# First mixer of a two-layer trunk: one adaLN unit with each product unit, in place of three with two

## The chip, the core and the metric

The kernel runs on one core of one Trainium2 chip. The metric is the device time of one execution in microseconds (us). Three timed executions of the kernel before took 2756.81, 2764.85 and 2773.1 us; the median, 2764.85 us, is the time before. A further execution was recorded by the hardware profiler, and every duration below is from it.

## The reference

The reference is a two-layer decoder trunk on one sequence of 256 tokens with 2048 channels, all in 32-bit floats. Each layer has a token mixer and a SwiGLU block, and each of these four sub-layers is

`x <- LayerNorm(ALPHA * x + (1 + gate(c)) * f(x * (1 + scale(c)) + shift(c)))`

The shift, scale and gate come from a conditioning vector c ("adaLN"):

```
mod = jax.nn.silu(c) @ w + b
shift, scale, gate = jnp.split(mod, 3, axis=-1)
```

For each sub-layer w has 2048 rows and 6144 columns, 48 MB in all, and is read once. The first layer's mixer (the "first mixer" here) projects its input to the columns of two head groups, an mLSTM group (8 heads of 128) and an RWKV-7 group (16 heads of 64), runs both recurrences, and sends their concatenated output through one more projection. The second layer's mixer does the same with retention and gated DeltaNet.

## The kernel before

**Product units.** Every large projection is cut into products of 512 output columns, and a product into units. A unit is one 1 MB load of weights (128 partitions x 2048 floats, 8 KB in each partition) into a tile called raw. Both halves of the tile are then split into two parts of reduced precision: ScalarE writes the high part hi (line 713), VectorE subtracts it to get the low part lo (line 714). TensorE multiplies hi and lo with the activations, split likewise, in 24 matmuls of 512 columns per unit (lines 728 to 730, eight of each). A mixer product has four units. `raw_p` has three tiles and the hi and lo parts have three buffers each.

**adaLN units.** The 48 MB of each adaLN matrix is cut into 48 units of 1 MB, 192 for the four sub-layers, numbered 0 to 191. A unit is the weights of 128 output columns, transposed. Its computation is one VectorE instruction on the whole tile (line 649), which multiplies it with silu(c) and sums along each row. So an adaLN unit costs one load of 1 MB and one long VectorE instruction, and neither ScalarE nor TensorE. Where an adaLN unit's tile is taken from is set by `self.homes`. In the first mixer this is `("raw",)`: the adaLN units share the three raw tiles with the weights of the products. In the later stages they go to two tiles of their own, za and zt (FFN), or alternate between za and raw (second mixer).

**Where adaLN units are put.** After each product unit `product` calls `fill(rate)`:

```
self.ada_credit = getattr(self, "ada_credit", 0.0) + rate
while self.ada_credit >= 0.999 and self.ada_next < self.ada_limit:
    self.ada(1)
    self.ada_credit -= 1.0
```

So `rate` is the number of adaLN units per product unit, up to a limit on their number. Units 0 to 31 (shift and scale of the first sub-layer) are read in `first_products`, before the mixer. In `mixer_ab` the limit is 80: it reads units 32 to 47 (the first gate) and 48 to 79 (shift and scale of the second sub-layer). The gate is first needed by `gate_rows` in `mix_out`, the others by `norm` at its end; both call `ada` for whatever is still missing by then.

**The first mixer.** `mixer_ab` has twelve products of four units, 48 product units. Eight of them belong to `rwkv` and its callback `after`: four give the remaining columns of the RWKV heads, four give columns for the first four mLSTM heads, which are put by in DRAM ("by", line 1151) and fetched again (line 1158). Between them four batches of RWKV heads run, each with a chain of small VectorE steps (the inverse, lines 1012 to 1024) and small matmuls; the fourth goes side by side with the first mLSTM group. The last four products belong to the second mLSTM group, a generator that `mix_out` steps through before its own products with `o_ab`, whose rate is 0.

**Order.** The Python order of the calls is the program order. Within a pool, tiles are opened in the order of the program. At the end of `body` a planner (`Plan`) simulates the engines with estimated costs and writes one fixed order for each engine, the loads on SyncE's queue included: among the instructions that could start it takes the one with the smallest priority, which is its place in the program, less an advance of 2000 for a weight's load and split. All of this is done when the program is built.

Of the kernel before, what the change touches and what calls it, by code (L numbers as in the profile page):

```python
# [1895 lines left out]
def body(tc, ins, out):  # L1896
    with ExitStack() as stack:
        k = Trunk(tc, ins, out, stack)
        k.setup()
        k.ada_limit = 32  # L1900
        h, early = k.first_products()
        x = (ins["x"], None)
        k.ada_limit = 80
        side = k.mixer_ab(h, 48.0 / 32, early)
        x, h = k.mix_out(ins["o_ab"], x, 0, side)
        x, h = k.ffn(0, x, h)
        k.ada_limit = 176
        k.mixer_cd(h, 32.0 / 44)
        x, h = k.mix_out(ins["o_cd"], x, 2)
        k.ffn(1, x, h)  # L1910
        plan = Plan(tc, tc.nc, 250, k.after)
        plan.prepare(0)
        order, _ = plan.run([x.bass_priority for x in plan.ins])
        plan.impose(order)
# [18 lines left out]
```

## Time and profile before

| | before |
|---|---|
| timed runs, median (lowest to highest) | 2764.85 us (2756.81 to 2773.1) |
| the profiled execution's own time | 2755.91 us |
| span of its instructions | 2754.2 us |
| TensorE (PE) busy | 2627.3 us, 95% |
| VectorE (DVE) busy | 2005.0 us, 73% |
| ScalarE (ACT) busy | 1272.4 us, 46% |
| mean granted TensorE clock | 0.982 |

The profile is a page of one execution. It gives the busy time of each engine, that of 40 slices of the span, the chain of work that ended last, and groups of instructions: source line, engine, operation, output<-inputs by tile name, count, busy time, the mean duration in ns, and the idle time of the engine just before. The trace behind it answers questions on a stretch of time: the busy time of each engine (windows), who waited for whom (waits), and the instructions that touch a tile. PE is TensorE's matmuls, PEld its weight loads, SPq SyncE's queue of loads. Matmuls overlap, so a busy PE need not be a PE at its peak.

### The profile page before, as it was taken

The numbers are of one execution on the slowest core, as the hardware profiler recorded it, in microseconds if no ns is written. First come the engines' busy times: TensorE is split into PE (matmuls) and PEld (weight loads), VectorE is DVE, ScalarE is ACT, GpSimd is POOL, SyncE is SP. The second block draws the span as 40 slices with busy tenths as digits, with TensorE's granted clock in tenths as the row PEclk, the third lists the DMA queues.
The fourth block names the chain that finished last, engine by engine and source line by source line (L and its number), as shares of the span: only waits on it lengthen the run. The fifth ranks groups of instructions, "written<-read, shape, count | busy, mean of one in ns | idle before, by whom it ended". The sixth has DMA issues, their size and how long they took to land.

```text
span 2754.2 us, 33686 instructions
## 1 busy us (share of the span) xinstructions
PE 2627.3 (95%) x12906; PEld 2155.3 (78%) x12906; DVE 2005.0 (73%) x3153; ACT 1272.4 (46%) x1706; POOL 76.8 (3%) x88
## 2 busy tenths in 40 slices
PE   5598999999999999999999999999999999999997
PEld 3476777788788888888888888888778888888886
DVE  7899887658777777767767989875866664557457
ACT  2364545557644444434446654444354444443442
POOL 0000100110000000000000101000000000000000
PEclk9899999999999999999999999999999999999999
DMA  9988775226578888778856776665657675556554
GB/s 394 358 297 300 253 287 207 92 93 211 202 302 303 311 320 315 286 251 309 311 194 227 272 282 220 259 231 204 226 200 274 259 271 188 196 213 240 192 186 165
DMA packets 109819, 681.60 MB, mean 247 GB/s; under 512 B 12437, under 2 KB 15705, under 8 KB 31577
## 3 DMA queue, kind: packets, MB, share of 16 engines
q1 hardware_dynamic: 108506, 677.36, 67.0%
q8 instruction: 101, 1.65, 0.2%
q10 hardware_dynamic: 1152, 2.10, 0.2%
q14 instruction: 60, 0.49, 0.0%
HBM read 668.89 MB, written 10.52 MB: 247 GB/s over the span
## 4 chain that ended last, share of the span: by engine, by line
PE 75%; DVE 6%; issue 3%; DMA 3%; ACT 2%; POOL 0%; DVEq 0%; SPq 0%; ACTq 0%; POOLq 0%
PE g L730 23%; PE g L728 23%; PE g L729 23%; DVE lo L714 1%; PE m L974 1%; ACT hi L713 1%; DMA t<-x 1%; DMA t<-lnrow 1%; DMA za<-ada 1%; DVE raw L649 0%; PE m L1254 0%; PE m L909 0%; PE c L1432 0%; DVE t L870 0%; DMA raw<-w_ab 0%
## 5 line engine op out<-in xcount | busy, mean ns | idle before, releaser
L714 DVE TENSOR_TENSOR lo<-raw,hi 128x1024 fp32r<-128x1024 f32 (+2 forms) x802 | 972.4, 1215 | 594.1 <-ACT hi L713 589.6
L713 ACT ACTIVATE hi<-raw 128x1024 fp32r<-128x1024 f32 (+2 forms) x802 | 842.3, 1053 | 1117.1 <-PE g L730 1028.5
L728 PE MATMUL g<-hi,h 128*128 128x512 f32 (+2 forms) x2312 | 908.8, 394 | 53.7 <-ACT h L792 39.5
L729 PE MATMUL g<-lo,h 128*128 128x512 f32 (+2 forms) x2312 | 907.0, 392 | 4.6 <-DVE lo L714 4.6
L730 PE MATMUL g<-hi,h 128*128 128x512 f32 (+2 forms) x2312 | 905.7, 392 | 0.0
L728 PEld LDWEIGHTS g<-hi,h 128*128 128x128 f32 x2312 | 439.3, 190 | 148.4 <-ACT h L792 42.4
L729 PEld LDWEIGHTS g<-lo,h 128*128 128x128 f32 x2312 | 440.2, 190 | 97.1 <-DVE lo L714 8.8
L730 PEld LDWEIGHTS g<-hi,h 128*128 128x128 f32 x2312 | 439.6, 190 | 86.6 <-issue 2.0
L728 PE MATMUL g<-hi,a 128*128 128x512 f32 x920 | 361.0, 392 | 5.8 <-DVE t L870 5.8
L729 PE MATMUL g<-lo,a 128*128 128x512 f32 x920 | 359.9, 391 | 0.5 <-DVE lo L714 0.5
L730 PE MATMUL g<-hi,a 128*128 128x512 f32 x920 | 359.8, 391 | 0.0
L728 PEld LDWEIGHTS g<-hi,a 128*128 128x128 f32 x920 | 173.4, 189 | 42.1 <-DVE t L870 6.3
L729 PEld LDWEIGHTS g<-lo,a 128*128 128x128 f32 x920 | 173.5, 189 | 36.2 <-DVE lo L714 0.9
L730 PEld LDWEIGHTS g<-hi,a 128*128 128x128 f32 x920 | 173.4, 188 | 35.8
L649 DVE SCALAR_TENSOR_TENSOR raw<-raw,silu_c 128x2048 f32<-128x2048 f32 x82 | 187.4, 2286 | 16.5 <-DMA raw<-ada 8.7
L649 DVE SCALAR_TENSOR_TENSOR za<-za,silu_c 128x2048 f32<-128x2048 f32 x56 | 127.9, 2284 | 3.5 <-DMA za<-ada 3.5
L649 DVE SCALAR_TENSOR_TENSOR zt<-zt,silu_c 128x2048 f32<-128x2048 f32 x38 | 86.8, 2284 | 1.4 <-DMA zt<-ada 1.4
L1438 DVE SCALAR_TENSOR_TENSOR f<-c,cols_sb,f 128x253 f32<-128x253 f32 (+2 forms) x120 | 56.1, 475 | 3.0 <-ACT f L1435 2.4
L1639 POOL TENSOR_SCALAR s<-cons_sb,log_alpha 128x128 f32<-128x128 f32 x16 | 15.9, 1006 | 1008.6 <-DVE log_alpha L1583 867.6
L649 DVE SCALAR_TENSOR_TENSOR a<-a,silu_c 128x2048 f32<-128x2048 f32 x16 | 36.4, 2286 | 0.2
L912 ACT ACTIVATE t<-m,affine 128x128 f32<-128x128 f32 x96 | 34.9, 470 | 0.1
L1254 PE MATMUL m<-y 64*128 64x256 f32 x128 | 30.6, 413 | 3.6 <-DVE a L1257 3.4
(480 smaller groups left out, 2095.7 us busy)
## 6 DMA issues: line engine op xcount, KB each, us to landing
raw<-gu SPq DMA_DIRECT2D x176, 1024.0 KB, 4.7
raw<-dn SPq DMA_DIRECT2D x88, 1024.0 KB, 4.8
raw<-ada SPq DMA_DIRECT2D x82, 1024.0 KB, 5.4
raw<-w_cd SPq DMA_DIRECT2D x60, 1024.0 KB, 4.8
za<-ada SPq DMA_DIRECT2D x56, 1024.0 KB, 7.0
raw<-w_ab SPq DMA_DIRECT2D x48, 1024.0 KB, 5.0
zt<-ada SPq DMA_DIRECT2D x38, 1024.0 KB, 6.9
a<-ada SPq DMA_DIRECT2D x16, 1024.0 KB, 17.0
```

What stands on the lines that cost most here:

```text
L649: v.scalar_tensor_tensor(w[:], w[:], 1.0, self.sc[:], ALU.mult, ALU.mult, accum_out=m[:, i:i + 1])
L713: nc.scalar.activation(hi[:, :2 * n], ws, AF.Copy)
L714: nc.vector.tensor_tensor(lo[:, :2 * n], ws, hi[:, :2 * n], ALU.subtract)
L728: mm(o, ah, wh, start=start and k == 0, stop=False)
L729: mm(o, ah, wl, start=False, stop=False)
L730: mm(o, al, wh, start=False, stop=stop and k == 3)
L912: nc.scalar.activation(h32[:, j, :], b[:, P * j:P * j + P], AF.Identity, bias=self.ab[:, sub + 1, 16 + k:17 + k], scale=self.ab[:, sub + 1 ...
L974: nc.tensor.transpose(b[:, P * k:P * k + P], gs[:, t, P * k:P * k + P], self.ident)
L1254: mm(b[:, T * x:T * x + T], bk[r, c, x, t, :], ar[r, c, t].rearrange("p x s -> p (x s)"), start=True, stop=True)
L1438: v.scalar_tensor_tensor(o[:, d:T], b[:, T * j:T * j + T - d], self.col(wname, 4 * (tile0 + i + j) + 3 - d), o[:, d:T], ALU.mult, ALU.add)
L1639: nc.gpsimd.tensor_scalar(L[:], sl, self.gl[:, t, 4 * g + j:4 * g + j + 1], None, ALU.mult)
```

## The change

One number in `body`: the rate at which the first mixer takes adaLN units goes from 48/32 to 48/48. Before, 1.5 units stand behind each of the first 32 product units (the first eight products), and none behind the other 16. After, one unit stands behind each of the 48 product units. The limit of 80, the tiles, the loads and the computation are the same, and the rates of the later stages are not touched. The planner makes its order anew.

```diff
         k.ada_limit = 80
-        side = k.mixer_ab(h, 48.0 / 32, early)
+        side = k.mixer_ab(h, 48.0 / 48, early)
         x, h = k.mix_out(ins["o_ab"], x, 0, side)
```

## The prediction

> **What bounds the kernel now.** I read the page first, then, since the change touches one stage only, the stretches of that stage.
>
> ```profile
> PE 2627.3 (95%) x12906; PEld 2155.3 (78%) x12906; DVE 2005.0 (73%) x3153; ACT 1272.4 (46%) x1706; POOL 76.8 (3%) x88
> ...
> GB/s 394 358 297 300 253 287 207 92 93 211 202 302 303 311 320 315 286 251 309 311 194 227 272 282 220 259 231 204 226 200 274 259 271 188 196 213 240 192 186 165
> ```
>
> TensorE is busy for 95% of the span, so over the whole kernel only 5% (127 us) is idle. The traffic is uneven: the third to sixth of the 40 slices (138 to 413 us) move 253 to 300 GB/s, the eighth and ninth (482 to 620 us) 92 and 93. Which products lie where, and which adaLN units, is told by two rows of groups of lines, from 140.8 to 447.2 us and from 447.2 to 620 us, and by the loads of the two tensors:
>
> ```profile
> L730 PE MATMUL g<-hi,h 128*128 128x512 f32 x256 | 104.7, 409 | 0.0
> ...
> L649 DVE SCALAR_TENSOR_TENSOR raw<-raw,silu_c 128x2048 f32<-128x2048 f32 x46 | 105.0, 2283 | 6.1 <-DMA raw<-ada 5.9
> L649 DVE DVE_READ_ACCUMULATOR raw<-raw,silu_c 128x1 f32 x46 | 3.7, 81 | 0.0
> ...
> L730 PE MATMUL g<-hi,h 128*128 128x512 f32 x128 | 52.1, 407 | 0.0
> ```
> ```profile
> L690 SPq DMA_DIRECT2D raw<-ada x48: 327/328/360, 124.2 to 433.1; - x48
> L690 SPq DMA_DIRECT2D raw<-w_ab x48: 327/328/371, 120.7 to 588.9; - x48
> ```
>
> A product unit has eight matmuls of line 730, so the first stretch ("early") holds 32 product units, the first eight products, and the second ("late") the other 16. All 48 adaLN loads are issued by 433.1 us, 46 of them computed in the early stretch, none in the late. How the two stretches stand, cut finer, with a stretch of the FFN below for comparison:
>
> ```profile
> core 0: us, PE busy (x) PEld busy (x) DVE busy (x) ACT busy (x) POOL busy (x), PEclk, DMA share, GB/s
> 140.80:192.00 51.20, 49.18 (x232) 37.96 (x231) 46.37 (x87) 32.09 (x52) 0.00 (x0) 1.00 0.84 294
> 192.00:262.00 70.00, 59.47 (x251) 44.37 (x250) 64.66 (x129) 28.52 (x46) 5.85 (x5) 0.95 0.83 309
> 262.00:315.00 53.00, 52.07 (x405) 41.84 (x404) 44.16 (x94) 25.48 (x53) 6.32 (x5) 1.00 0.69 248
> 315.00:385.40 70.40, 64.94 (x393) 50.15 (x392) 65.92 (x140) 33.45 (x54) 0.79 (x2) 0.98 0.82 296
> 385.40:447.20 61.80, 59.34 (x309) 45.38 (x307) 43.24 (x113) 27.05 (x58) 4.38 (x5) 0.94 0.60 217
> 447.20:485.90 38.70, 37.70 (x307) 30.89 (x308) 28.35 (x85) 25.18 (x40) 0.00 (x0) 1.00 0.56 190
> 485.90:523.00 37.10, 32.68 (x171) 24.16 (x170) 22.85 (x93) 17.02 (x47) 7.33 (x11) 0.87 0.10 29
> 523.00:555.00 32.00, 32.00 (x171) 27.23 (x170) 25.65 (x67) 22.28 (x33) 0.00 (x0) 0.99 0.48 165
> 555.00:617.00 62.00, 60.92 (x452) 50.90 (x451) 37.12 (x109) 29.62 (x57) 7.57 (x12) 1.00 0.29 103
> ...
> 140.80:447.20 306.40, 285.01 (x1584) 219.71 (x1582) 264.34 (x559) 146.58 (x262) 17.34 (x16) 0.97 0.76 274
> 447.20:617.00 169.80, 163.29 (x1097) 133.18 (x1098) 113.97 (x353) 94.11 (x175) 14.89 (x23) 0.97 0.34 118
> ...
> 826.00:1500.00 674.00, 670.33 (x3051) 555.49 (x3050) 490.60 (x548) 302.25 (x343) 0.00 (x0) 1.00 0.76 281
> ```
>
> Early, PE idles 306.4 - 285.0 = 21.4 us and DVE is 86% busy (92 to 94% in the two stretches of 70 us); late, PE idles 6.5 us and DVE is 67% busy. What PE waits for early is in the waits:
>
> ```profile
> PE g L728 <- ACT hi L713: 10.3, 6, 3.0
> PE g L729 <- DVE lo L714: 3.0, 6, 0.5
> PE m L1254 <- DVE a L1257: 3.0, 4, 1.9
> PE c L1202 <- DVE za L1105: 1.4, 2, 1.1
> PE m L1028 <- DVE y L1024: 1.1, 2, 1.0
> PE g L728 <- ACT zt L1131: 1.1, 1, 1.1
> ...
> ACT hi L713 <- DMA raw<-w_ab: 44.2, 13, 8.8
> ```
>
> Half of it is products waiting for a split (10.3 + 3.0 us), and the split in turn waits for its weights (13 times, 44.2 us). That is the three raw tiles, which weights and adaLN units share, not the DMA engines, which are 83% busy where it is worst. From 192 to 262 us the loads were:
>
> ```profile
> L690 SPq DMA_DIRECT2D raw<-ada x12: 327/328/328, 197.3 to 259.0; - x12
> L690 SPq DMA_DIRECT2D raw<-w_ab x8: 327/328/328, 193.3 to 251.7; - x8
> ```
>
> Twenty loads in 70 us are one in 3.5 us; with three tiles each is held for 10.5 us, and three tiles in five carry adaLN.
>
> **The change, part by part.** *Removed early:* 16 of the 48 adaLN units, each a 1 MB load, a turn of a raw tile, 0.33 us of SP's queue and 2.28 + 0.08 = 2.37 us of DVE, 37.9 us of DVE in all. What of it reaches PE is a price that no row shows; I bound it by the waits.
>
> (a) Waits of products for splits, 10.3 + 3.0 + 1.1 = 14.4 us. The eight weights of 192 to 262 us would bring 8 adaLN loads, not 12: 16 loads at 3.5 us are 56 us, 14 us below the 70, against 10.5 us of idle PE there. So the tile turns no longer hold PE, but the chains of the RWKV batches still do; I take two thirds, -9.6 us, of ends 0 and -14.4.
>
> (b) Clock. 1 - PEclk times the length gives 3.5 us lost in 192 to 262 and 1.4 us in 315 to 385.4, the two stretches with the heaviest adaLN load. (385.4 to 447.2 loses 3.7 us at a lighter load, so I leave it.) Half of 4.9: -2.5 us, of ends 0 and -4.9. The Trainium skill, TensorE: Matmul & The Clock Gate, "What's actually happening", has the clock fall to half after an idle window of some 3.4 us. The longest early wait in the rows is 3.0 us, and the clock fell to 0.95 all the same, so the trace does not bear it out here; the rule alone would put (b) at 0, and the sum 2.5 us higher.
>
> (c) RWKV matmuls waiting for DVE, 3.0 + 1.4 + 1.1 = 5.5 us. A third of the long instructions that they can stand behind goes: -1.8 us, of ends 0 and -5.5.
>
> *Added late:* the same 16 units, spread by the product units. The matmuls of line 730 place them:
>
> ```profile
> 447.20:485.90 38.70, 12.63 (x32) 6.03 (x32) 1.00 0.56 190
> 485.90:523.00 37.10, 3.83 (x9) 1.80 (x8) 0.87 0.10 29
> 523.00:555.00 32.00, 14.01 (x36) 6.72 (x35) 0.99 0.48 165
> 555.00:617.00 62.00, 20.03 (x49) 9.23 (x49) 1.00 0.29 103
> ```
>
> 32, 9, 36 and 49 by eight are 4, 1, 4.5 and 6 units. DVE then has 28.35 + 9.5 = 37.8 of 38.7 us, 22.85 + 2.4 = 25.2 of 37.1, 25.65 + 10.7 = 36.3 of 32.0, and 37.12 + 14.2 = 51.3 of 62.0. (d) Only the third overflows, by 4.3 us; nine loads at 3.5 us would fit there (31.5 us). I take +4. The others have DVE's idle time as cover; without it a unit costs its 2.37 us. Behind the long instruction the splits (line 714) and the steps of the last RWKV batch wait, and PE for these; the end where all 16 lie on that path is +37.9, the other 0.
>
> (e) SP's queue. It is in order, and stood still in the second stretch:
>
> ```profile
> SPq L1158 <- PE c L1329: 43.9, 1, 43.9
> ...
> 467.21 6.23 SPq L690 DMA_DIRECT2D raw<-w_ab  x2
> 517.41 2.13 SPq L1158 DMA_DIRECT2D q<-by  x4
> 526.80 2.88 SPq L690 DMA_DIRECT2D raw<-w_ab  x2
> ...
> raw<-w_ab SPq DMA_DIRECT2D x48, 1024.0 KB, 5.0
> ```
>
> A fetch of the columns put by waits for its tile for 43.9 us, and all loads behind it. The weights that landed before are PE's filler meanwhile. With an adaLN unit between two weights the three tiles hold one product unit less, so the next weight leaves behind the fetch, at 519.5 us (517.41 + 2.13), and lands 5.0 us later at 524.5, to be split then; before, PE was busy without a break from 523 us. +2 us, of ends 0 and +5 (one such landing).
>
> *Not touched.* Gate and second shift and scale are complete after 48 of 48 product units, and nothing is left to catch up before the rows of the gate or the norm. The last adaLN load stands ahead of the first weights of the output projection in SP's queue and the tiles; in 555 to 617 us the DMA engines are 29% busy, which covers it (0.33 us of queue, or 3.5 us if a tile turn shows).
>
> Sum: -9.6 - 2.5 - 1.8 + 4 + 2 = -7.9, about -8 us. The profiled execution, 2755.9 us, becomes 2747.8; it lies 8.9 us below the median of the runs shown, so on that median the forecast is 2764.85 - 8 = 2757 us. What this measurement can tell from no change is 0.5%, 14 us.
>
> **The rivals.** *Hidden anyway* (2765 us). The early stretch is paced by PE's own work and the RWKV chains, and the waits return elsewhere; early PE is 93% busy, and of its 21.4 idle us only 14.4 have to do with the splits. Against it speaks that DVE is above 92% busy in the two stretches where PE idles most.
>
> *The tile turns pace the whole early stretch.* Busy PE isn't PE at its peak: weight loads are busy 219.7 / 306.4 = 72% early, 133.2 / 169.8 = 78% late and 82% in the FFN. If early rose to the late share it would last 219.7 / 0.784 = 280 us, -26; with +6 late, -20: 2745 us. By the tile turns alone 192 to 262 gives 14 us, and 315 to 385.4 with its 393 PE instructions a like amount, which agrees. Against it speaks the small idle time of PE: 21.4 us early, of which 10.5 in 192 to 262. The Trainium skill, Perfetto Trace Analysis, "Identifying the Most-Contended Engine", calls weight-load share, not matmul busy share, the measure of headroom; that is this rival.
>
> *DVE pays late, on the other side.* The late stretch has the inverse chain of the fourth RWKV batch, the mLSTM convolutions and the splits on DVE, all in one order that cannot give way; a unit started between two steps of a chain holds it for 2.37 us. With all 16 on the path and the early gain of 13.9: +37.9 + 2 - 13.9 = +26, 2791 us. It decides against the change from (13.9 + 14) / 2.37 = 12 of the 16 units on; with 6 it is even. For it speaks the third late stretch, 80% busy before anything is added; against it the 33% of idle DVE late.
>
> *It doesn't do what it says:* the planner could leave the units where they were. Tiles are opened in program order, and the loads of 192 to 262 us follow it (12 to 8), so the early tiles must lose them; but a plan made anew can move everything by some us either way.
>
> **How the numbers follow.** Forecast, -18 to +2 about -8: 0.43, of which 0.12 below -14. Hidden anyway: 0.15, all within 14 us. Tile turns: 0.20, all faster. DVE late: 0.19, of which 0.17 slower than +14. Not as said, or another plan: 0.03, counted as same 0.01, slower 0.02. Faster by over 0.5%: 0.12 + 0.20 = 0.32; slower 0.17 + 0.02 = 0.19; within 0.5% 0.49. The range leaves out a tenth on each side: -26, the full tile-turn gain early, and +18, two thirds of the way to the DVE case: 2739 to 2783 us. The forecast's own range is 2747 to 2767.
>
> **What would show it.** Loads of adaLN until about 585 us, 32 of them before the ninth product. Early: the stretch of the first eight products shorter than 306 us by about 14, the 44.2 us of splits waiting for weights cut by more than half, DVE near 228 us busy. Late: 16 long DVE instructions, and the last four products longer than 170 us by about 6. The forecast is wrong if the early stretch keeps its length though those waits are gone (hidden anyway), if it drops by 25 us or more (tile turns), or if the late stretch grows by more than 20 us with PE waiting for DVE (the last rival).

## The result, and the profile after

| | before | after |
|---|---|---|
| median of 4 runs each (lowest to highest) | 2768.01 us (2756.81 to 2773.1) | 2733.59 us (2730.63 to 2734.41) |
| ratio to before, 95% interval | | 0.9884 [0.9853, 0.9914] |
| the profiled execution's own time | 2755.91 us | 2733.0 us |
| mean granted TensorE clock there | 0.982 | 0.984 |

The kernel became 1.2% faster: 34 us between these medians, 27 us against the median of the 81 runs of the kernel before that were made beside the experiments (2761 us), 23 us between the two profiled executions. The forecast was 2757 us, its range 2739 to 2783: the time lies 5 us below the range.

The page of the kernel after, engines and traffic:

```profile
span 2731.3 us, 33687 instructions
...
PE 2616.0 (96%) x12906; PEld 2151.6 (79%) x12906; DVE 2007.7 (74%) x3153; ACT 1273.4 (47%) x1706; POOL 73.0 (3%) x88
...
GB/s 394 365 242 272 247 224 232 202 160 218 214 316 308 314 317 309 284 245 317 294 214 215 288 240 254 251 234 201 226 213 272 254 262 196 185 214 248 187 188 165
```

The instructions are the same in number, and the hole of 92 and 93 GB/s in the eighth and ninth slice is filled (202 and 160). Where the units lie now is shown by the tile view (loads of adaLN, and the weights of the products) and by two rows each of the groups of lines, first those of 140.5 to 416.7 us, then those of 416.7 to 599.3 us:

```profile
L690 SPq DMA_DIRECT2D raw<-w_ab x48: 327/328/618, 119.6 to 562.4; - x48
L690 SPq DMA_DIRECT2D raw<-ada x48: 327/328/353, 123.1 to 578.9; - x48
```
```profile
L730 PE MATMUL g<-hi,h 128*128 128x512 f32 x256 | 102.3, 399 | 0.0
L649 DVE SCALAR_TENSOR_TENSOR raw<-raw,silu_c 128x2048 f32<-128x2048 f32 x31 | 70.8, 2285 | 8.3 <-DMA raw<-ada 8.2
...
L730 PE MATMUL g<-hi,h 128*128 128x512 f32 x128 | 53.5, 418 | 0.0
L649 DVE SCALAR_TENSOR_TENSOR raw<-raw,silu_c 128x2048 f32<-128x2048 f32 x16 | 36.5, 2284 | 6.0 <-DMA raw<-ada 5.9
```

Loads go on until 578.9 us, 31 long instructions lie in the first eight products, 16 in the last four: the change does what it says. The two stretches, in the columns that the prediction quoted (length, PE, PEld, DVE, ACT, POOL busy, clock, DMA share, GB/s):

```profile
140.50:416.70 276.20, 270.54 (x1586) 215.09 (x1584) 235.94 (x544) 148.17 (x264) 14.40 (x16) 1.00 0.68 247
416.70:599.30 182.60, 170.09 (x1124) 138.50 (x1122) 144.65 (x371) 97.92 (x180) 17.85 (x25) 0.95 0.55 197
```

I cut both kernels at the first matmul of the first, of the ninth and behind the last of the twelve products. Before, that gives these rows:

```profile
140.80:447.30 306.50, 285.04 (x1585) 219.75 (x1583) 264.40 (x560) 146.68 (x262) 17.34 (x16) 0.97 0.76 274
447.30:620.90 173.60, 167.16 (x1120) 136.54 (x1121) 116.06 (x356) 97.88 (x179) 17.11 (x25) 0.97 0.34 116
```

A stretch is PE's busy time and its idle time, and what the throttle costs is counted in the busy time, as (1 - clock) times the length. The rows print the clock to two places; for the losses I used the trace's unrounded clock, so 8.5 us early before, where 0.03 x 306.5 would give 9.

| us | early before | early after | late before | late after |
|---|---|---|---|---|
| length | 306.5 | 276.2 (-30.3) | 173.6 | 182.6 (+9.0) |
| PE idle | 21.5 | 5.7 (-15.8) | 6.4 | 12.5 (+6.1) |
| lost to the clock | 8.5 | 0.0 (-8.5) | 5.1 | 8.5 (+3.4) |
| the rest: PE busy at full clock | 276.5 | 270.5 (-6.0) | 162.1 | 161.6 (-0.5) |

Early and late together are 21.3 us of the 22.9 us between the two profiled executions. The idle time that went is that of the splits. The waits of the kernel after, early: the row that answers to 44.2 us, and what PE still waits for:

```profile
ACT hi L713 <- DMA raw<-w_ab: 13.0, 6, 3.6
...
PE c L1202 <- DVE e L1021: 1.4, 1, 1.4
...
PE g L729 <- DVE lo L714: 1.1, 2, 0.5
PE m L1254 <- DVE a L1257: 1.0, 3, 0.7
...
PE m L1080 <- DVE y L1072: 0.5, 1, 0.5
PE c L1231 <- DVE f L1229: 0.5, 2, 0.2
...
PE c L1202 <- DVE za L1105: 0.3, 1, 0.3
```

Products waiting for a high part (10.3 us before) don't appear among PE's waits any more, and splits wait 13.0 us for weights in place of 44.2. The weights are late because the loads in SP's queue wait for a raw tile, most of all for one that a long adaLN instruction still holds (early, before and then after):

```profile
SPq L690 <- DVE raw L649: 59.7, 17, 10.8
```
```profile
SPq L690 <- DVE raw L649: 45.3, 9, 7.3
```

So the turns of the tiles and DVE's time are one chain. Late, the fetch in SP's queue waits 17.8 us where it waited 43.9 (first row, the queue's waits), and PE's longest wait is one behind DVE (second row, the waits of the engines):

```profile
SPq L1158 <- PE c L1329: 17.8, 1, 17.8
```
```profile
PE c L1202 <- DVE za L1105: 3.6, 1, 3.6
```

### The profile page after: what moved, and what is told of

Same layout as the page of the kernel before. It is cut to its first block, busy times and chain, and to the rows that moved or that the text cites. A ratio compares the mean times of both kernels' runs of the same rounds, so it can differ in the third digit from the quotient of the medians.

```text
span 2731.3 us, 33687 instructions
## 1 busy us (share of the span) xinstructions
PE 2616.0 (96%) x12906; PEld 2151.6 (79%) x12906; DVE 2007.7 (74%) x3153; ACT 1273.4 (47%) x1706; POOL 73.0 (3%) x88
## 4 chain that ended last, share of the span: by engine, by line
PE 81%; DMA 8%; DVE 7%; ACT 2%; issue 2%; SPq 0%; POOL 0%; DVEq 0%; ACTq 0%
PE g L728 24%; PE g L729 24%; PE g L730 24%; DMA raw<-ada 3%; DVE lo L714 2%; DVE raw L649 1%; DMA za<-ada 1%; DMA y<-w_ab 1%; ACT hi L713 1%; DMA t<-x 1%; PE m L974 1%; DMA t<-lnrow 1%; DMA raw<-w_ab 0%; PE m L1254 0%; DMA zt<-ada 0%
## 5 line engine op out<-in xcount | busy, mean ns | idle before, releaser
L1095 POOL TENSOR_SCALAR_AFFINE_SELECT a<-a 128x512 f32<-128x512 f32 (+1 forms) x20 | 23.3, 1175 | 316.1 <-ACT a L1256 293.0
```

Source lines behind the costliest of these rows:

```text
L1095: self.nc.gpsimd.affine_select(x, x, pattern=[[0, n] for n in dims] + [[1, P]], compare_op=ALU.is_gt if strict else ALU.is_ge, fill=0.0, b ...
```

## The experiments

Each kernel is the one before with the edit shown, unless it says otherwise; the numbers of the change itself stand in the first two rows. The ratio is to the runs of the kernel before that were made beside each kernel on the same chip; the kernel after has only the four runs of the result. "Both" is the early and the late stretch together, from one profiled execution. In the kernels marked * the order moves other work across the ninth product (some 1850 matmuls early in place of 1585), so their early stretch can't be compared. The last column is the median over all runs of the time less (1 - mean granted clock) x span; I call it the steady time.

| kernel | median us (lowest to highest) | ratio to before [95%] | early us: idle, clock | both us: idle, clock | steady us |
|---|---|---|---|---|---|
| before (81 runs) | 2761.2 (2750 to 2776) | | 306.5: 21.5, 8.5 | 480.2: 27.9, 13.7 | 2703.9 |
| after | 2733.6 (2731 to 2734) | 0.988 [0.985, 0.991] | 276.2: 5.7, 0.0 | 458.8: 18.2, 8.5 | 2687.8 |
| e1_half_dve | 2754.3 (2749 to 2763) | 0.997 [0.996, 0.999] | 304.0: 18.3, 11.9 | 477.2: 24.3, 17.1 | 2701.4 |
| e2_half_load | 2820.0 (2815 to 2822) | 1.021 [1.019, 1.024] | 340.4: 46.5, 25.6 | 540.2: 53.5, 56.3 | 2725.6 |
| e3_rooms | 2773.8 (2772 to 2776) | 1.005 [1.003, 1.007] | 296.4: 17.5, 5.1 | 467.0: 22.9, 8.5 | 2715.6 |
| e4_fourth_tile | 2781.1 (2775 to 2789) | 1.008 [1.005, 1.011] | 302.8: 19.9, 10.2 | 475.9: 25.8, 15.4 | 2709.3 |
| e5_half_priced* | 2753.9 (2733 to 2767) | 0.996 [0.993, 0.999] | | 481.9: 16.6, 32.4 | 2689.6 |
| e6_priced_only* | 2769.7 (2754 to 2771) | 1.002 [1.000, 1.005] | | 492.5: 31.5, 25.6 | 2704.7 |
| e9_half_load_priced | 2755.5 (2747 to 2760) | 0.997 [0.995, 0.999] | 310.3: 25.2, 11.9 | 474.6: 26.7, 13.7 | 2700.3 |
| e7_no_adaln* | 2718.4 (2714 to 2721) | 0.986 [0.984, 0.987] | | 441.4: 6.5, 3.4 | 2676.1 |
| e8_early_alone | 2729.9 (2724 to 2734) | 0.989 [0.988, 0.991] | 280.9: 6.7, 3.4 | 452.4: 10.6, 8.5 | 2682.2 |
| e12_late_alone | 2801.1 (2791 to 2807) | 1.012 [1.008, 1.016] | 322.1: 21.5, 25.6 | 530.2: 39.0, 58.0 | 2707.4 |
| e10_rate_48_24* | 2760.1 (2755 to 2765) | 0.999 [0.997, 1.000] | | 482.2: 31.6, 13.7 | 2705.4 |
| e11_rate_48_40 | 2767.0 (2752 to 2778) | 1.001 [0.999, 1.004] | 300.9: 12.5, 17.1 | 484.7: 23.7, 27.3 | 2696.5 |
| e16_spread_5_2 | 2748.1 (2747 to 2751) | 0.996 [0.994, 0.998] | 290.6: 14.1, 5.1 | 463.3: 18.8, 10.2 | 2698.0 |
| e15_rate_48_44 | 2740.3 (2729 to 2743) | 0.992 [0.990, 0.995] | 283.8: 10.4, 3.4 | 461.8: 19.5, 10.2 | 2689.4 |
| e13_price_before | 2754.1 (2744 to 2758) | 0.998 [0.997, 1.000] | 300.2: 16.7, 8.5 | 478.2: 21.0, 20.5 | 2697.0 |
| e14_price_after | 2758.1 (2746 to 2762) | 0.998 [0.996, 1.000] | 282.9: 5.9, 6.8 | 478.2: 19.6, 29.0 | 2694.7 |
| e17_price2_before | 2744.8 (2740 to 2749) | 0.994 [0.992, 0.997] | 295.1: 16.9, 6.8 | 466.6: 23.1, 10.2 | 2698.0 |
| e18_price2_after | 2736.7 (2732 to 2743) | 0.992 [0.990, 0.995] | 279.8: 5.7, 3.4 | 462.4: 15.9, 13.7 | 2686.1 |

How far can the last column be trusted? A run's mean clock is on record to three places, which is 2.8 us of its steady time. The steady times of the 81 runs before lie between 2695.9 and 2711.8 us (standard deviation 3.3 us), and their medians on the five chips used between 2702.5 and 2705.0. Against the 81 runs a kernel's steady time is known to 1 to 6 us (95%), e12_late_alone's to 12; between two kernels of four runs each, a difference of 5 or 6 us can hardly be told from none.

### DVE's time, or the loads and tiles?

Both were named early: DVE over 92% busy where PE idles most, and three raw tiles held 10.5 us each. Two kernels take half of one away and leave the rate. In the first, the long instruction of units 32 to 79 sums only 1024 of the 2048 columns:

```diff
-        v.scalar_tensor_tensor(w[:], w[:], 1.0, self.sc[:], ALU.mult, ALU.mult, accum_out=m[:, i:i + 1])
+        c = D // 2 if 32 <= u < 80 else D
+        v.scalar_tensor_tensor(w[:, :c], w[:, :c], 1.0, self.sc[:, :c], ALU.mult, ALU.mult, accum_out=m[:, i:i + 1])
```

> The kernel before with its rate of 48/32, but the long VectorE instruction of each adaLN unit of the first mixer (units 32 to 79) reads only half of the columns (1024 of 2048); the loads and the tiles stay as they are, and half of each sum is left out of the result. VectorE's work early falls by 48 x 1.06 = 51 us, more than the 37.9 us that the change moved away. If VectorE's long instructions were what the change relieved (theory V), the time falls by as much as the change gave early or more: 30 us, about 2738 us. If it was the turns of the raw tiles (theory T), a turn of an adaLN unit is shorter by 1.06 of 10.5 us in three turns out of five, 6%: 5 to 10 us, about 2760 us.

In the second, the same units load half the bytes and go over them twice, so the other half of the columns is left out:

```diff
-            w = self.raw(src)
+            w = self.raw(src[:, :D // 2] if 32 <= u < 80 else src)
...
+            v.scalar_tensor_tensor(w[:, :c], w[:, :c], 1.0, self.sc[:, c:], ALU.mult, ALU.mult, accum_out=m[:, i:i + 1])
+            v.scalar_tensor_tensor(w[:, :c], w[:, :c], 1.0, self.sc[:, :c], ALU.mult, ALU.mult, accum_out=m[:, i:i + 1])
```

> The kernel before with its rate of 48/32, but each adaLN unit of the first mixer loads only half of its columns (512 KB), and VectorE works twice on this half, so that its time per unit stays (2 x 1.23 us); the other half is left out of the result. 24 MB less are moved early. V: no gain, 2768 us. T: the load's part of a turn falls from 4.8 us to perhaps 3.5 us in three turns out of five, 7 or 8%: 5 to 10 us less, about 2760 us. If it was the traffic itself that slowed the weights (theory D), 24 MB less are more than the 16 MB that the change moved: 30 us, about 2738 us.

The row of the first, early, against 264.40 us of DVE and 285.04 of PE before:

```profile
140.60:444.60 304.00, 285.69 (x1584) 222.02 (x1582) 216.94 (x559) 146.81 (x262) 13.10 (x16) 0.96 0.76 276
```

DVE lost 47 us of work and the stretch 2.5 us; the time lies nearer to theory T's 2760 us than to V's 2738. But both kernels have a flaw, which the second makes plain: at half the bytes it took 56 us longer, which no theory expected, with 46.5 us of PE idle early. The planner prices a long instruction at a fixed 2373 ns (line 309). In the first it went on planning for the long one, so the short one ran in the old order; in the second it counted two such prices and made an order for twice the DVE time. Neither is a clean price of the resource.

So the two were made again with the price of the short instruction, 1275 ns, and a third kernel has that price alone, with the full instruction:

```diff
-                if x.is_scalar_tensor_tensor:
+                if x.name in CHEAP:
+                    d = 1275
+                elif x.is_scalar_tensor_tensor:
```

> The kernel before with its rate of 48/32; as in the run with half the columns, the long VectorE instruction of the first mixer's adaLN units takes 1.23 us in place of 2.28 us (half of each sum is left out of the result), and this time the planner is also given a price of 1.275 us for it, not 2.373 us, so that it makes its order for the short instruction. Theory V2 (VectorE's time early is what the change relieved, but by way of the order that the planner makes for it): about 25 us less than before, 2740 us. Theory T (tiles) or D (traffic): loads and turns are the same, no more than 5 to 10 us less, as in the run with half the columns.

> The kernel before with its rate of 48/32 and nothing left out; only the planner's price for the long VectorE instruction of the first mixer's adaLN units is 1.275 us in place of 2.373 us. The order is that of the run with half the columns and the short price, the instruction still takes 2.28 us. If the order alone set the time, this run would gain what that run gains (25 us, 2740 us). If VectorE's time itself is short as well (V2), the long instructions come late against this order: 0 to 15 us less than before, 2750 to 2765 us. T and D: no gain.

> The run with half of the bytes once more, since its planner charged each of the two short VectorE instructions 2.373 us, so that its order was made for twice the VectorE time; now it is charged 1.275 us each, 2.55 us per unit, near the 2.46 us that they take. Rate 48/32, half of the columns left out of the result, 24 MB less moved early. V2 (VectorE's time, by way of the order): the same VectorE time, so the same as before, 2755 to 2768 us. D (the traffic): 30 us less, 2735 us. T: 5 to 10 us less.

Half the DVE time with an order to match takes 14 us off the steady time (2703.9 to 2689.6), nearly as much as the change (16); the same order with the full instruction takes off nothing (2704.7; its median is 5 us above the 2750 to 2765 expected), and the short instruction in the old order 2.5 us. So DVE's time counts, by way of an order that uses it: in the twelve products, less the clock, the same order takes 449.5 us with the short instruction and 466.9 with the full one. (A shorter instruction also gives its tile back 1 us sooner.) In most runs the clock took part of it back: e5_half_priced lost 44 to 77 us to it, and its median is 14 us above the 2740 that was expected. Half the bytes, priced right, takes off 3.6 us of steady time, and its median is at the 2755 to 2768 us that V2 expected, not at the 2735 of the theory of traffic. And e2_half_load and e9_half_load_priced, the same instructions under two prices, lie 65 us apart.

The tiles were tested by one more of them. I found no room for a fourth of 8 KB, so every second unit goes to a tile of 7 KB (1792 of 2048 columns; the rest is left out), for which two pools of small tiles give up a buffer; the control gives up the buffers alone and computes everything:

```diff
-        return self.mix.tile(shape, F32, tag="t2", bufs=3, name=self.name("t"))
+        return self.mix.tile(shape, F32, tag="t2", bufs=2, name=self.name("t"))
...
-        sg = self.own([P, NT, T], "b2", 3)
+        sg = self.own([P, NT, T], "b2", 2)
```
```diff
+        elif home == "zx":
+            w = self.own([P, D - 256], home, 1)
+            src = src[:, :D - 256]
...
+        k.homes = ("zx", "raw")
```

> The kernel before with its rate of 48/32 and one buffer less in two small pools (t2 and b2, two instead of three), which makes room for the next run. It is only that run's comparison. All theories: the same as before or somewhat slower, 2768 to 2790 us.

> The run with fewer small buffers, and in the room gained a tile of 7 KB for every second adaLN unit of the first mixer, the rate still 48/32; the last 256 columns of these units are left out of the result. Tiles for 2.5 loads per product unit go from three to four, VectorE's work and the bytes stay but for one part in 16. T: most of what the change gave early comes, 20 to 30 us less than the run with fewer small buffers. V and D: no more than 5 us less.

With the tile the splits wait 29.1 us for weights early (first fence), without it 33.1 (second), and the steady time is 6 us lower; the median is 7 us higher, since 11 us more go to the clock.

```profile
ACT hi L718 <- DMA raw<-w_ab: 29.1, 7, 7.3
```
```profile
ACT hi L713 <- DMA raw<-w_ab: 33.1, 11, 7.5
```

But the 6 us are not in the twelve products, where alone the tile is used. Less the clock these take 460.5 us with the tile and 458.5 without (from the table: both stretches less their clock). The difference lies behind them: less the clock, 2131.0 us with the tile and 2138.8 without. So by this test another tile was worth nothing here, against the 20 to 30 us of theory T. The test is a weak one: the tile is smaller and takes only half of the units, every edit brings another order, and both kernels lost small buffers, which cost 12 us of steady time. That cost, too, lies behind the twelve products (2133.3 us before, 2166.3 in the control, by the spans); within them the control, at the same rate as the kernel before, was 8 us shorter less the clock.

### What the units cost, early and late

Three kernels leave units out or add some. In the first, from the kernel after, units 32 to 79 are zeros and the first mixer reads no adaLN; in the second, also from the kernel after, units 64 to 79 are zeros, so that there are 32 units early and none late; the third computes everything, as the kernel before, and adds 16 units late whose sums nobody uses:

```diff
+        left = 32 <= u < 80
...
+        if left:
+            v.memset(self.mod[:, i:i + 1], 0.0)
```
```diff
+        left = 64 <= u < 80
```
```diff
+        self.filled = getattr(self, "filled", 0) + 1
+        if 32 < self.filled <= 48:
+            w = self.raw(self.ins["ada"][31 + self.filled])
+            self.nc.vector.scalar_tensor_tensor(w[:], w[:], 1.0, self.sc[:], ALU.mult, ALU.mult, accum_out=self.spare[:, self.filled - 33:self.filled - 32])
```

> The kernel after with all 48 adaLN units of the first mixer left out of the work and of the result: no load, no long VectorE instruction, a short one that writes zero in its place. It gives what the adaLN units cost at all. All theories: less than before by what they cost at 48/32. If the rate of 48/48 had nearly removed that cost, this run lies no more than 10 us below the kernel after (2725 us); if it took only a part of it, 20 us or more below it (2710 us).

> The kernel after with the 16 adaLN units that stand in the last four products left out (units 64 to 79, out of the result too). It is the change's early part alone. If the early gain of 30 us and the late cost of 9 us in the two traces stand by themselves, this run lies 9 us below the kernel after (2725 us) with an early stretch of 276 us and a late one of 172 to 174 us.

> The kernel before with its rate of 48/32, and 16 adaLN units of the last four products added to it: units 64 to 79 are loaded and computed a second time there, into a tile that nothing reads. It is the change's late part alone, at its full price, with nothing taken away early. If the late cost in the two traces stands by itself: 9 us slower than before, 2773 us, with the late stretch 182 us long. If a late unit costs its whole 2.37 us: 38 us slower, 2800 us.

In steady time: without any units 2676.1; 32 early 2682.2 (+6 for 32); 32 early and 16 late 2687.8 (+6 for the last 16); 48 early 2703.9 (+22 for 16 more early); 48 early and 16 more late 2707.4 (+3.5 for 16 late). The late price is 4 to 6 us for 16 units from two sides, near the +6 of the forecast, but in steady time neither can be told from nothing (4.9 us by the means both times, give or take 6 and 12). The full price, 37.9 us, is excluded. The early price is not even: the first unit behind each product unit costs little (6.8 us by the means for 32, give or take 6), the 16 units more that the kernel before takes there cost 1.4 us each, or some 0.9 to 1.0 by the orders at other prices below (2697.0 and 2698.0 at 48/32). By the medians the 16 late units cost 4 us in one kernel and 40 in the other, and nearly all of the 40 is clock (94 us lost over the run in place of 55), so that e12_late_alone came out at the 2800 us expected of the full price for another reason. Of the other two expectations neither was met as it stands: e7_no_adaln lies 15 us below the kernel after, between its two cases, and e8_early_alone 4 us, not 9 (early 280.9 us, late 171.4). The late row of e12_late_alone:

```profile
463.00:671.10 208.10, 190.65 (x1122) 154.34 (x1121) 151.55 (x392) 98.83 (x182) 15.99 (x25) 0.84 0.49 178
```

### Other rates

All compute everything. Only the rate differs; the fourth has 1.25 units with each product unit of the first eight products and 0.5 with those of the last four.

```diff
-        side = k.mixer_ab(h, 48.0 / 32, early)
+        side = k.mixer_ab(h, 48.0 / 24, early)
```
```diff
+        side = k.mixer_ab(h, 48.0 / 40, early)
```
```diff
+        side = k.mixer_ab(h, 48.0 / 44, early)
```
```diff
-            banks = product(10 + i)
+            banks = self.product([w[4 * (10 + i) + k] for k in range(KG)], 512, h, 0.5)
...
+        side = k.mixer_ab(h, 1.25, early)
```

> The kernel before with a rate of 48/24: two adaLN units with each of the first 24 product units, none with the other 24. VectorE's work is moved the other way, into the first six products. V2 and T: slower than before, by 10 to 20 us (2775 to 2785 us), with more idle time of TensorE in the first six products. If the time went by which order the planner happens to find (theory P), either sign.

> The kernel before with a rate of 48/40: 1.2 adaLN units with each of the first 40 product units, that is 38 in the first eight products and 10 behind. V2 and T: between before and after, 2740 to 2755 us. P: either side, also slower than before.

> A rate of 48/44, 1.09 adaLN units with each of the first 44 product units: 35 in the first eight products, 13 behind. If the idle time of TensorE follows VectorE's load early: time without the clock's loss 2690 to 2696 us, between 48/40 (2698) and 48/48 (2689), and by the clock 2735 to 2755 us. P: outside of this.

> Two rates: 40 adaLN units in the first eight products (1.25 with each product unit) and 8 in the last four (0.5), so that they reach the mixer's end as in the kernel after, with half as many moved. If idle time follows the load early: time without the clock's loss 2694 to 2700 us, 2740 to 2758 us by the clock. If what counts is that the units reach the end of the mixer, as after: 2735 us.

In steady time the rate runs in one direction: 2705.4 at 48/24, 2703.9 at 48/32, 2696.5 at 48/40 (2698.0 at 1.25 and 0.5), 2689.4 at 48/44, 2687.8 at 48/48. The two ends (48/24 and 48/32, 48/44 and 48/48) can't be told apart, and each rate has one order here. The medians don't run so: 2760, 2761, 2767 (2748), 2740, 2734. At 48/40 the clock cost 55 to 89 us in a run. The 10 to 20 us expected at 48/24 did not come, 48/40 missed its range by the clock, and the medians of the other two lie within theirs.

### The same change in other orders

Nothing so far told the rate from the order that the planner makes with it. So its price of the long instruction, an estimate that changes no instruction, was moved by about 1% down and up, and the change was made under each price:

```diff
-                    d = 2373 if len(x.outs) > 1 or n >= 2048 else 150 + n * 1.045 + (55 if n > 100 else 5)
+                    d = 2344 if len(x.outs) > 1 or n >= 2048 else 150 + n * 1.045 + (55 if n > 100 else 5)
```
```diff
+                    d = 2400 if len(x.outs) > 1 or n >= 2048 else 150 + n * 1.045 + (55 if n > 100 else 5)
```

> The kernel before (48/32) with another order: the planner's price for every adaLN instruction is 2.344 us, not 2.373 us; nothing else is changed and nothing left out. With the next run it asks whether the gain belongs to the rate or to one order that the planner happened to find. If to the rate: within 8 us of the kernel before, 2752 to 2770 us. If to an order (P): anything, the gain of the pair (this run against the next) may be gone.

> The kernel after (48/48) with the same other price, 2.344 us. If the gain belongs to the rate: 20 to 35 us below the run at 48/32 with this price, 2728 to 2745 us. P: it may lie near that run.

> The kernel before (48/32) with a third order: the planner's price for every adaLN instruction is 2.400 us. Nothing else is changed. If the rate gives its early gain in every order and the rest is the order: within 15 us of the kernel before, 2745 to 2775 us, with an early stretch of 298 to 307 us.

> The kernel after (48/48) with the price of 2.400 us. If the early gain belongs to the rate, its early stretch is 15 to 30 us shorter than that of the run at 48/32 with this price. If the whole gain belongs to the rate and the order at 2.344 us was the unlucky one, the time is 2730 to 2740 us; if it was the kernel after that had the lucky order, 2745 to 2765 us.

Early and late rows at 2344 ns, 48/32 and then 48/48:

```profile
140.10:440.30 300.20, 283.46 (x1586) 221.04 (x1584) 266.82 (x569) 147.61 (x264) 13.05 (x16) 0.97 0.76 279
440.30:618.30 178.00, 173.71 (x1121) 142.26 (x1120) 113.61 (x346) 96.90 (x178) 17.16 (x25) 0.93 0.33 114
```
```profile
139.50:422.40 282.90, 276.95 (x1584) 220.81 (x1583) 236.76 (x540) 149.01 (x265) 14.37 (x16) 0.98 0.67 242
422.40:617.80 195.40, 181.77 (x1124) 147.55 (x1122) 144.85 (x378) 96.90 (x180) 17.86 (x25) 0.89 0.50 184
```

and at 2400 ns:

```profile
140.20:435.30 295.10, 278.23 (x1585) 219.00 (x1584) 264.33 (x574) 145.90 (x263) 12.07 (x16) 0.98 0.77 284
435.30:606.80 171.50, 165.26 (x1123) 135.38 (x1122) 113.96 (x342) 97.31 (x178) 17.70 (x25) 0.98 0.35 119
```
```profile
141.10:420.90 279.80, 274.13 (x1585) 217.70 (x1583) 236.41 (x546) 148.36 (x264) 14.33 (x16) 0.99 0.67 244
420.90:603.50 182.60, 172.39 (x1124) 138.88 (x1121) 144.34 (x371) 97.51 (x180) 18.24 (x25) 0.94 0.55 196
```

The products' waits for splits, early, at 2344 ns (48/32, then 48/48) and at 2400 ns (the same two):

```profile
PE g L728 <- ACT hi L713: 7.4, 4, 2.8
PE g L729 <- DVE lo L714: 4.7, 8, 0.8
```
```profile
PE g L729 <- DVE lo L714: 1.0, 2, 0.5
...
PE g L728 <- ACT hi L713: 0.3, 1, 0.3
```
```profile
PE g L728 <- ACT hi L713: 7.8, 4, 2.9
PE g L729 <- DVE lo L714: 3.2, 5, 0.8
```
```profile
PE g L729 <- DVE lo L714: 1.3, 2, 0.8
```

| price of the long instruction | early | PE idle early | steady time | clock loss | median |
|---|---|---|---|---|---|
| 2373 ns (the change) | -30.3 | 21.5 to 5.7 | -16 | -9 | -27 |
| 2344 ns | -17.3 | 16.7 to 5.9 | -2 | +6 | +4 |
| 2400 ns | -15.3 | 16.9 to 5.7 | -12 | +1 | -8 |

(Each column has its own medians, so they don't add up exactly.) In all three the early stretch gets shorter and nearly all its idle time goes: that belongs to the rate. The products' waits for splits go with it: 14.4 to 1.1, 12.1 to 1.3, 11.0 to 1.3 us. How much it gets shorter, and what is left in the end, does not belong to the rate alone. The order of the kernel before is the poorest of the three at its rate (early 306.5 against 300.2 and 295.1 us), that of the kernel after has the shortest early stretch of the three at its own (276.2 against 282.9 and 279.8). At 2344 ns the late stretch takes back the gain (178.0 to 195.4 us, at a clock of 0.89), and what follows the twelve products, which the change doesn't touch, is longer too: 2762.2 - 617.8 = 2144.4 us against 2755.1 - 618.3 = 2136.8 us by the profiled executions' own times.

Take the clock's loss off each stretch, and the three pairs fall into place:

| us less the clock's loss | early | late | behind the twelve products |
|---|---|---|---|
| 2373 ns (the change) | 298.0 to 276.2 (-21.8) | 168.5 to 174.0 (+5.5) | 2117.2 to 2119.2 (+2.0) |
| 2344 ns | 291.6 to 276.1 (-15.5) | 166.1 to 173.1 (+7.0) | 2117.8 to 2126.4 (+8.7) |
| 2400 ns | 288.3 to 276.4 (-11.8) | 168.1 to 172.4 (+4.3) | 2118.8 to 2116.3 (-2.5) |

At 48/48 the early stretch is the same in all three orders; what differs there is the clock alone (0.0, 6.8 and 3.4 us). At 48/32 it differs by 10 us between orders, in idle time and in PE's busy time at full clock. The late price is 4 to 7 us in all three. So within the twelve products the change gains in every order, 16, 9 and 8 us less the clock; the part behind them and the clock decide what is left.

Of the expectations, e13_price_before and e18_price2_after were met; e14_price_after, which was to lie 20 to 35 us below its partner, was not; and e17_price2_before was just outside its own (2744.8 against 2745 us, early 295.1 against 298). No kernel that computes everything had a lower median than the one after.

## Why the prediction was wrong

For the kernel measured the direction and the mechanism held, the size did not. Of the 23.4 us between the forecast and the median, 3.7 are its base (2764.85 us by three runs, 2761.2 by 81), 4.7 are that the profiled execution before lay further below its kernel's median (5.3 us) than the one after (0.6), and 15.0 are the sum's: -7.9 us forecast, -22.9 between the two profiled executions. (2755.9 - 7.9 is 2748.0, not 2747.8; nothing rests on it.) By the steps of the forecast, on these two:

**(a) Products waiting for splits, -9.6 us forecast, 0 to -14.4.** Of the 14.4 us, 1.1 us are left: -13.3 us, and -10.8 and -9.7 in the pairs at the other prices. The waits let go, as worked out, and in this pair the chains of the RWKV batches did not keep their third. That it was the number of tiles is not shown (a fourth one gave nothing); DVE's time, which holds them, counted by itself.

**(b) Clock, -2.5 us forecast, 0 to -4.9.** Early lost 8.5 us before and nothing after; late 5.1 and then 8.5. This term was mis-sized, beyond its far end: I had left out the 3.7 us of 385 to 447 us because the adaLN load is lighter there, and halved the rest. The loss doesn't follow the load in that way, and in the pairs at the other prices it went down by 1.7 and 3.4 us early, and up by 10.3 and 6.8 late. In the two traces it goes with PE's waits: in the early stretch of the kernel before, all four stretches of half clock begin during or within 2 us behind a wait of 1.6 to 3.0 us; in that of the kernel after no wait is longer than 1.4 us, and there is no half clock. That is a link, not a test, and the last section shows half clock with hardly a wait ahead of it.

**(c) RWKV matmuls waiting for DVE, -1.8 us forecast.** All rows of such waits come to 6.0 us before (the 5.5 and one of 0.5) and to 1.4 + 1.0 + 0.5 + 0.5 + 0.3 = 3.7 us after: -2.3 us. Together (a) and (c) make up 15.6 of the 15.8 us of idle time that went.

**What had no term.** 6.0 us of early PE time at full clock went too, for the same matmuls (4.8 and 0.7 us at the other prices). I took it for PE's own work. By the prediction's own sign, an early stretch shorter by 25 us or more, this is the size of the rival of the tile turns. By the share of weight loads it had early at 280 us: it was 276.2, and the share is 215.09 / 276.20 = 78%, that of the late stretch before (282.9 and 279.8 us at the other prices, 78% too). The Trainium skill, Perfetto Trace Analysis, "Identifying the Most-Contended Engine", prefers that share to busy PE as a sign of headroom, and the trace agrees on the size. It does not say what fills the room. The rival's own mechanism, tiles that pace the stretch, got nothing from the fourth tile in these products, and in the other orders the stretch shrank by 17.3 and 15.3 us, near the 13.9 us of the forecast's (a) to (c).

**(d) and (e), the late stretch, +6 us forecast.** +9.0 us measured: 6.1 us of idle time, 3.4 of clock. Less the clock the late stretch grew by 5.5, 7.0 and 4.3 us in the three pairs. So the last rival but one (DVE pays late, 37.9 us) is out in the steady time. Within the sum the split is less sure: the fetch in SP's queue, behind which I put (e), waits 17.8 us and not 43.9, and PE's one long wait is on DVE (3.6 us).

**The step that failed.** Three terms of the sum were too small: the clock (-8.5 us early, beyond the far end of -4.9), PE's busy time at full clock, which had no term at all (-6.0), and the waits for splits (-13.3 in place of -9.6). Behind the three stands one assumption: the sum was made as though the order stayed what it was and the 16 units were lifted out of it. The rival that says otherwise, "a plan made anew can move everything by some us either way", got a chance of 0.03, none of it on the faster side. The three pairs have the same change at -27, +4 and -8 us; in steady time at -16, -2 and -12, around a forecast of -5.4 (the -7.9 without the clock's -2.5), and the clock adds -9, +6 and +1. In the twelve products alone, less the clock, two of the pairs give -9 and -8, close to these -5.4; the pair that was measured gives -16, because its order at 48/32 was the poorest of the three. So a part of the large gain is luck of the order. Medians at 48/32 differ by 16 us between orders, at 48/48 by 24. A forecast from the waits of one order can give the part that belongs to the rate, but the range had to carry, on each side, about half of the 16 to 24 us by which orders at one rate differ. That much this study shows. Which feature of an order makes it poor at 48/32, and what sets the clock in it, stays open. A true fourth raw tile of 8 KB was not tried.

## What to carry to other kernels

Where a program plans a fixed order, every edit is two edits: the one in the text and a new order. Before a gain of 1% is put down to the first, make the same edit under a neighbouring plan (move a price of the planner by 1%, which changes no instruction) and see how much of it stays; here that was between nothing and all. When a PE-bound stretch is read, take idle time, clock and PE's busy time at full clock apart, and don't take busy PE for work that can't shrink.

## What the runs showed of the hardware

**The clock makes most of the spread between runs.** The kernel before lost 44 to 72 us to it in 81 runs; their times have a standard deviation of 5.7 us, and of 3.3 us once it is taken off. The fastest and the slowest run of e5_half_priced lie 35 us apart, its steady times no more than 11. A difference of some us between medians is safer read with the clock's loss beside it.

**Half clock lasts while PE is busy.** In the profiled execution of e12_late_alone one stretch of half clock lasted 41 us. Its windows, before, in and behind it:

```profile
380.00:391.40 11.40, 10.87 (x160) 8.82 (x159) 11.01 (x20) 6.98 (x16) 0.00 (x0) 1.00 0.78 285
391.40:432.40 41.00, 41.00 (x146) 32.82 (x145) 16.38 (x42) 11.30 (x26) 1.69 (x2) 0.50 0.39 142
432.40:440.00 7.60, 7.60 (x34) 4.96 (x34) 5.80 (x21) 4.18 (x11) 1.02 (x1) 1.00 0.15 57
```

PE is busy in all of the 41.0 us, and was for 10.87 of the 11.40 us ahead of them; by the rows of waits its longest wait from 380 to 434 us is 0.5 us:

```profile
PE m L1085 <- DVE y L1077: 0.5, 1, 0.5
```

The Trainium skill, TensorE: Matmul & The Clock Gate, "What's actually happening", has the clock go to half after an idle window of some 3.4 us and back after as much of sustained work. Neither fits these rows: no such idle window stands ahead, and 41 us of busy PE did not bring it back. The matmuls themselves confirm the record of the clock: those of one line and shape took 404 ns each in the first of these windows and 680 in the second.

```profile
L730 PE MATMUL g<-lo,h 128*128 128x512 f32 x8 | 3.2, 404 | 0.0
```
```profile
L730 PE MATMUL g<-lo,h 128*128 128x512 f32 x7 | 4.8, 680 | 0.0
```

In the kernel before, by contrast, half clock in the early stretch stands close behind waits. The first of the four stands behind one of 3.0 us:

```profile
210.00:223.50 13.50, 10.49 (x48) 7.90 (x46) 11.81 (x33) 4.86 (x8) 0.00 (x0) 1.00 0.62 234
223.50:226.90 3.40, 3.36 (x7) 2.25 (x8) 3.40 (x6) 0.82 (x1) 0.00 (x0) 0.50 0.78 272
```

What brings the clock down no run here shows.
